# Hybrid DeltaNet / short-conv layer: where block 0 keeps its modulation sums, its later modulation rows and its decay vectors

## The chip, the cores and the metric

One core of a Trainium2 chip runs the whole layer. The metric is the time of one execution on the device in microseconds (us), as the median of three runs. Engines are named as in the profile: PE (TensorE matmul), PEld (its weight load), DVE (VectorE), ACT (ScalarE), POOL (GpSimd) and SP (SyncE, which here only issues DMAs). "L158" is line 158 of the kernel before; "SPq" is SP's queue of DMA issues.

## The reference, cut to what matters

Sequence 2048, width 1024, one layer, float32. `c` is one conditioning row, and from it come six modulation rows:

```
mod = silu(c) @ w_ada + b_ada                      # (6 * 1024): shift, scale, gate for mixer and MLP
h = rmsnorm(x, pre_mix) * (1 + sc_m) + sh_m
proj = h @ w_in                                    # q,k,v,z of 4 heads, a, b, and three short-conv parts
q,k,v = silu(causal_conv4(.)); q,k l2-normed
g = -exp(dn_a_log) * softplus(a + dn_dt_bias); beta = sigmoid(b)
o = gated delta rule in chunks (triangular inverse per chunk, then a scan over chunks)
y = concat(rmsnorm(o) * silu(z), s_b * causal_conv3(s_c * s_h)) @ w_out
x = x + g_m * rmsnorm(y, post_mix)
h = rmsnorm(x, pre_ffn) * (1 + sc_f) + sh_f
x = x + g_f * rmsnorm(square(relu(h @ w_ff1)) @ w_ff2, post_ffn)
```

`w_ada` is 1024 x 6144, 25 MB: the six parts of 4 MB are shift, scale and gate of the mixer (parts 0, 1, 2) and of the MLP (parts 3, 4, 5).

## The kernel before, in words

The sequence is cut into four blocks of 512 tokens. Each block runs the opening norm with the transposition to feature-major (`pre_norm`, for block 0 `pre_norm_first`), the gating vectors (`gating`), the mixer (`mixer`, `mix_out`) and the MLP (`ffn`). Every matmul operand is split into a high and a low part (ACT casts the high part, line 246; DVE, sometimes POOL, subtracts for the low part, line 247), and each product is three matmuls (lines 332 and 337).

Weights of a projection pass through a staging tile `w1s` (`stage()`, three buffers of 512 KB), are split into `w1h` (three buffers) and used. In block 0 the split weights are also written to DRAM (`wc`), so that later blocks load them without a split.

The modulation exists only in block 0. There `silu(c) @ w_ada` is not a matmul at first: 128 rows of `w_ada` at a time are scaled by the column of `c_act` that belongs to them and summed on DVE, eight tiles to one sum (lines 127/129 and 156/158), and the sum over the 128 partitions is then taken by matmuls with a vector of ones (line 168, in `ada_affine`) or a matrix of ones (line 188, in `ada_gate`).

- Parts 0 and 1 are read in four quarters of 256 features (`ada_load`, line 146): quarters 0 and 2 into `sb` tiles, 1 and 3 into `w1h` tiles. `ada_first` sums a quarter in a `t2` tile. `t2` has four buffers, and the copies of `h` on their way to the split (line 268, released by line 272 on POOL) rotate through the same four. After each quarter `ada_affine` makes scale and shift, `to_hT` transposes two 128-feature tiles of `x`, and `proj` takes these two tiles into the accumulators of the four projections that are begun early (`EARLY`, 96 matmuls in all). The 16 matmuls of `gating` (lines 443, 445) come after.
- Parts 2, 4 and 3 are read in the mixer by `ada_acc`, eight rows of 512 KB each, through the same three `w1s` buffers as the projection weights (line 125); their sums live in `gate_m`, `gate_f` and one `sb` tile. Part 5 follows in the MLP of block 0, group 1.

The decay vectors `dn_a_log` and `dn_dt_bias` and the 8 columns of `w_in` for a and b are loaded from SP's queue behind the x tiles and the first two quarters (lines 371, 374, 377). `neg_a` (lines 485, 486) is computed from the first.

The chunk inverse in the mixer is a chain of 60 DVE instructions (lines 635, 637) between line 630 and line 640; its result goes through DRAM (`rd`) to the tile `comp`, from which `block_inverse` (matmuls of lines 667 to 689) starts, and then the scan.

`w2h` (pool `opnd`, three buffers of 512 KB) holds split `w_out` weights in `mix_out`, and in the MLP of block 0, groups 1 and 2, the pairs of `w_ff2` rows from which `weight_sums` makes sums for DRAM (lines 901 to 907). `wt` (pool `small`, two buffers) is a tile of `block_inverse`.

Buffers, semaphores and the order of instructions on each engine are set by a planner from the program order and its own estimate of times: an instruction can be put well ahead of its place in the program if its inputs and a buffer are free by that estimate. Once set, each engine and SP's queue run in that order and wait in it.

Of the kernel before, what the change touches and what calls it, by code (L numbers as in the profile page):

```python
# [8 lines left out]
F32 = mybir.dt.float32  # L9
F32R = mybir.dt.float32r  # L10
# [5 lines left out]
P = 128  # L16
SEQ = 2048
DM = 1024
KT = DM // P
DFF = 4096  # L20
TB = 512
NB = SEQ // TB
NT = TB // P
NH = 4
# [4 lines left out]
OFF_Z, OFF_AB, OFF_SB, OFF_SC, OFF_SH = 1536, 2048, 2056, 2568, 3080  # L29
# [3 lines left out]
def hybrid_layer(  # L33
# [21 lines left out]
    nc = tc.nc  # L55
    V, A, G, T = nc.vector, nc.scalar, nc.gpsimd, nc.tensor
    x, out = x[0], out[0]
    w_ada, w_in, w_out, w_ff1, w_ff2 = w_ada[0], w_in[0], w_out[0], w_ff1[0], w_ff2[0]

    const = ctx.enter_context(tc.tile_pool(name="const", bufs=1))  # L60
    big = ctx.enter_context(tc.tile_pool(name="big", bufs=1))
    opnd = ctx.enter_context(tc.tile_pool(name="opnd", bufs=2))
    work = ctx.enter_context(tc.tile_pool(name="work", bufs=2))
    small = ctx.enter_context(tc.tile_pool(name="small", bufs=2))
# [12 lines left out]
    def slot_a(dtype=F32):  # L77
        return big.tile([P, 1024], dtype, name="sa", bufs=15)

    def slot_b(dtype=F32):  # L80
        return big.tile([P, 1024], dtype, name="sb", bufs=7)

    def t2():
        return work.tile([P, TB], F32, name="t2", bufs=4)

    def stage():
        return work.tile([P, 1024], F32, name="w1s", bufs=3)

    def junk(n, ph):
        return work.tile([P, n], BF16, name="jk_" + ph, bufs=1)  # L90

# [29 lines left out]
    def ada_acc(part, acc):  # L121

        for k in range(KT):
            st = stage()
            nc.sync.dma_start(out=st, in_=w_ada[k * P:(k + 1) * P, part * DM:(part + 1) * DM])
            if k == 0:
                V.tensor_scalar(out=acc, in0=st, scalar1=c_act[:, 0:1], scalar2=None, op0=ALU.mult)
            else:
                V.scalar_tensor_tensor(out=acc, in0=st, scalar=c_act[:, k:k + 1], in1=acc,
                                       op0=ALU.mult, op1=ALU.add)  # L130
        return [acc[:, 0:TB], acc[:, TB:DM]]

    def ada_load(qd):

        if qd % 2:
            sts = []
            for _ in range(2):
                w = opnd.tile([P, 2, KT, P], F32R, name="w1h", bufs=3).bitcast(F32)
                w = w.rearrange("p a k f -> p a (k f)")
                sts += [w[:, 0], w[:, 1]]  # L140
        else:
            sts = [slot_b() for _ in range(4)]
        for k0, st in zip(range(0, KT, 2), sts):
            for n in range(2):
                c0 = n * DM + qd * 256
                nc.sync.dma_start(out=st.rearrange("p (k n f) -> p k n f", k=2, n=2)[:, :, n],
                                  in_=w_ada[k0 * P:(k0 + 2) * P, c0:c0 + 256]
                                  .rearrange("(k p) f -> p k f", p=P))
        return sts

    def ada_first(sts):
        acc = t2()
        for k in range(KT):
            sj = sts[k // 2][:, (k % 2) * TB:(k % 2 + 1) * TB]
            if k == 0:
                V.tensor_scalar(out=acc, in0=sj, scalar1=c_act[:, 0:1], scalar2=None, op0=ALU.mult)
            else:
                V.scalar_tensor_tensor(out=acc, in0=sj, scalar=c_act[:, k:k + 1], in1=acc,  # L158
                                       op0=ALU.mult, op1=ALU.add)
        return [acc[:, 256:512], acc[:, 0:256]]  # L160
# [67 lines left out]
    def meansq(src):  # L228
        s = small.tile([P, 1], F32, name="ss_w", bufs=8)
        A.activation(out=junk(DM, "w")[:, :src.shape[-1]], in_=src, func=AF.Square,  # L230
                     scale=float(DM) ** -0.5, accum_out=s)
        return s

    def load_x(b, t):
        t0 = b * TB + t * P
        xt = slot_a()
        nc.sync.dma_start(out=xt, in_=x[t0:t0 + P, :])
        return xt
# [113 lines left out]
    ]  # L352
    for r0, n, src in segs:
        nc.scalar.dma_start(out=rows[r0:r0 + n, :], in_=src)
    xn0 = [load_x(0, t) for t in range(NT)]
    quarters = [ada_load(0)]
    cols = const.tile([P, 109], F32, name="cols")
# [9 lines left out]
    dn_w = cols[:, 108:109]  # L367

    quarters.append(ada_load(1))
    alog = const.tile([P, NH], F32, name="alog")  # L370
    nc.sync.dma_start(out=alog, in_=dn_a_log.broadcast_to([P, NH]))
    neg_a = const.tile([P, NH], F32, name="neg_a")
    dtb = const.tile([P, NH], F32, name="dtb")
    nc.sync.dma_start(out=dtb, in_=dn_dt_bias.broadcast_to([P, NH]))

    wab_s = t2()[:, 0:64].rearrange("p (k f) -> p k f", k=KT)
    nc.sync.dma_start(out=wab_s, in_=w_in[:, OFF_AB:OFF_AB + 8].rearrange("(k p) f -> p k f", p=P))
    wab = const.tile([P, KT, 16], F32R, name="wab")
    V.tensor_copy(out=wab[:, :, 0:8], in_=wab_s)
    V.tensor_tensor(out=wab[:, :, 8:16], in0=wab_s, in1=wab[:, :, 0:8], op=ALU.subtract)  # L380
# [2 lines left out]
    for t in range(NT):  # L383
        A.activation(out=junk(DM, "w"), in_=xn0[t], func=AF.Square, scale=float(DM) ** -0.5,
                     accum_out=r0[:, 0, t:t + 1])
# [511 lines left out]
    def weight_sums(g, j, e, o):  # L897


        r0 = (g * GRP + 2 * j) * P  # L900
        nc.sync.dma_start(out=e, in_=w_ff2[r0:r0 + P, :])
        nc.sync.dma_start(out=o, in_=w_ff2[r0 + P:r0 + 2 * P, :])
        a, b = slice(0, TB), slice(TB, 2 * TB)
        V.tensor_tensor(out=e[:, a], in0=e[:, b], in1=e[:, a], op=ALU.subtract)
        V.tensor_tensor(out=e[:, b], in0=o[:, b], in1=e[:, b], op=ALU.subtract)
        V.tensor_tensor(out=o[:, b], in0=o[:, b], in1=e[:, a], op=ALU.subtract)
        V.tensor_tensor(out=o[:, a], in0=o[:, a], in1=o[:, b], op=ALU.subtract)
        for i, t in enumerate((e, o)):
            pend.append((sums[g][:, j, 2 * i:2 * i + 2, :], t.rearrange("p (i f) -> p i f", i=2)))

    def ffn(b, hT, x1d):
# [22 lines left out]
        for g in range(NG):  # L934
# [11 lines left out]
            def job():  # L946
                if jobs:
                    if g == 0:
                        e, o = slot_b(), slot_b()
                    else:  # L950
                        e, o = [opnd.tile([P, 2, TB], F32R, name="w2h", bufs=3).bitcast(F32)
                                .rearrange("p a f -> p (a f)") for _ in range(2)]
                    weight_sums(*jobs.pop(0), e, o)

            def relu2(ps, a, c0, c1):
# [44 lines left out]
            if b == 0 and g == 1:  # L1000
                ada_acc(5, ada["gate_f"])
# [43 lines left out]
            while jobs:  # L1045
                job()
# [4 lines left out]
            if g == NG - 1 and b == NB - 1:  # L1051
                combine()
                w2 = [[], []]
                for n in range(2):
                    ns = slice(n * TB, (n + 1) * TB)
                    for fp in range(HP):
                        r0 = (f0 + 2 * fp) * P
                        st = stage().rearrange("p (j f) -> p j f", j=2)
                        nc.sync.dma_start(out=st, in_=w_ff2[r0:r0 + 2 * P, ns]
                                          .rearrange("(j p) f -> p j f", p=P))  # L1060
                        for j in range(2):
                            i = n * GRP + 2 * fp + j
# [20 lines left out]
            if seven:  # L1083
                for an, bn, key in (("A11", "B11", "1"), ("S2", "T2", "6"), ("A12", "B21", "2"),
# [3 lines left out]
                    for d in range(HP // 2):  # L1088
# [8 lines left out]
                        for j in range(2):  # L1097
                            i = 2 * d + j
# [5 lines left out]
            else:  # L1104
                for n in range(2):
                    ns = slice(n * TB, (n + 1) * TB)
                    pss = [ps_acc() for _ in range(NT)]
                    for fp in range(HP):
                        r0 = (f0 + 2 * fp) * P
                        w = load_w2(w_ff2[r0:r0 + 2 * P, ns].rearrange("(j p) f -> p j f", p=P))  # L1110
                        for j in range(2):
                            f = 2 * fp + j
# [52 lines left out]
```

## Time and profile before

| | |
|---|---|
| median of 3 runs | 2547.3 us (2545.57 to 2550.13) |
| profiled execution, its own time | 2542.68 us |
| its span, first to last instruction | 2540.9 us |
| mean granted TensorE clock | 0.985 |
| PE busy | 2434.5 us (96%), 11874 matmuls |
| DVE / ACT / POOL busy | 1779.2 us (70%) / 1152.9 us (45%) / 225.2 us (9%) |
| DMA moved | 449.53 MB, mean 177 GB/s |

The profile is read from this one execution. PE's busy time is wide because matmuls are pipelined; where PE does nothing, something else sets the pace, so the table is read together with the stretches below: the busy time of each engine in a stretch, the granted clock, the share of the 16 DMA engines in use.

### The profile page before, as it was taken

The numbers are of one execution on the slowest core, as the hardware profiler recorded it, in microseconds if no ns is written. First come the engines' busy times: TensorE is split into PE (matmuls) and PEld (weight loads), VectorE is DVE, ScalarE is ACT, GpSimd is POOL, SyncE is SP. The second block draws the span as 40 slices with busy tenths as digits, with TensorE's granted clock in tenths as the row PEclk, the third lists the DMA queues.
The fourth block names the chain that finished last, engine by engine and source line by source line (L and its number), as shares of the span: only waits on it lengthen the run. The fifth ranks groups of instructions, "written<-read, shape, count | busy, mean of one in ns | idle before, by whom it ended". The sixth has DMA issues, their size and how long they took to land.

```text
span 2540.9 us, 33780 instructions
## 1 busy us (share of the span) xinstructions
PE 2434.5 (96%) x11874; PEld 2020.3 (80%) x11874; DVE 1779.2 (70%) x3833; ACT 1152.9 (45%) x2386; POOL 225.2 (9%) x391
## 2 busy tenths in 40 slices
PE   4886999999989999999999999999999999999998
PEld 3675887888868888888877898888887888888887
DVE  5677776777796568666688557856779556857675
ACT  4631563344555145544464244654455414654432
POOL 1312100000040110000002020000002020000000
PEclk8898999999999999999999999999999999999999
DMA  7378858975455642444556545155445554244453
GB/s 250 124 243 261 305 179 298 304 257 165 150 198 215 207 158 100 132 127 135 154 183 232 170 151 187 67 155 150 146 158 210 185 188 166 92 151 131 125 162 103
DMA packets 297268, 449.53 MB, mean 177 GB/s; under 512 B 39189, under 2 KB 195978, under 8 KB 282250
## 3 DMA queue, kind: packets, MB, share of 16 engines
q1 hardware_dynamic: 296912, 447.31, 53.6%
q8 instruction: 94, 1.54, 0.2%
q14 instruction: 76, 0.62, 0.1%
q10 hardware_dynamic: 186, 0.06, 0.0%
HBM read 376.01 MB, written 71.30 MB: 176 GB/s over the span
## 4 chain that ended last, share of the span: by engine, by line
PE 77%; DVE 13%; DMA 5%; ACT 3%; issue 2%; SPq 0%; ACTq 0%; POOL 0%; DVEq 0%
PE acc L332 43%; PE acc L337 24%; DVE t L435 2%; DVE w1h L247 1%; DMA w1s<-in_w_ada_dram 1%; PE pd L701 1%; DVE sa L506 1%; DMA w2h<-in_w_ff_dram 1%; PE pd L557 1%; PE pd L332 1%; PE tp L689 1%; DVE sb L847 1%; PE pd L715 1%; PE tp L677 1%; DVE t L158 1%
## 5 line engine op out<-in xcount | busy, mean ns | idle before, releaser
L332 PE MATMUL acc<-h,w1h 128*128 128x512 f32 x5184 | 1231.6, 394 | 18.2 <-ACT w1h L246 16.0
L332 PEld LDWEIGHTS acc<-h,w1h 128*128 128x128 f32 x5184 | 973.0, 189 | 218.4 <-ACT w1h L246 17.1
L337 PE MATMUL acc<-w1h,sa 128*128 128x512 f32 x2556 | 593.6, 391 | 3.9 <-ACT w1h L246 3.2
L337 PEld LDWEIGHTS acc<-w1h,sa 128*128 128x128 f32 x2556 | 478.6, 188 | 104.7 <-ACT w1h L246 3.6
L247 DVE TENSOR_TENSOR w1h<-w1s,w1h 128x1024 fp32r<-128x1024 f32 x333 | 406.8, 1222 | 146.8 <-ACT w1h L246 146.6
L246 ACT CAST w1h<-w1s 128x1024 fp32r<-128x1024 f32 (+1 forms) x343 | 359.1, 1047 | 308.6 <-PE acc L337 205.1
L957 DVE TENSOR_TENSOR t<-t 128x512 f32<-128x512 f32 (+1 forms) x148 | 91.4, 620 | 182.9 <-ACT t L956 180.1
L956 ACT ACTIVATE t<-acc 128x512 f32<-128x512 f32 (+1 forms) x132 | 73.8, 559 | 247.9 <-PE acc L332 247.5
L272 POOL TENSOR_TENSOR h<-t,h 128x256 fp32r<-128x256 f32 x70 | 56.4, 810 | 1250.4 <-ACT h L271 1245.7
L435 DVE SCALAR_TENSOR_TENSOR t<-cb,cols,t 128x512 f32<-128x512 f32 x144 | 118.7, 831 | 67.9 <-ACT t L433 65.8
L247 DVE TENSOR_TENSOR w2h<-sa,w2h 128x512 fp32r<-128x512 f32 x128 | 87.7, 687 | 38.6 <-ACT w2h L246 37.9
L332 PE MATMUL acc<-h,sa 128*128 128x256 f32 (+1 forms) x672 | 104.8, 313 | 7.2 <-ACT h L271 5.8
L332 PEld LDWEIGHTS acc<-h,sa 128*128 128x128 f32 x672 | 93.2, 199 | 15.6 <-ACT h L271 7.8
L246 ACT CAST w2h<-sa 128x512 fp32r<-128x512 f32 x128 | 78.4, 619 | 56.5 <-DVE w2h L247 35.4
L337 PE MATMUL acc<-w2h,sa 128*128 128x512 f32 x420 | 101.4, 393 | 0.0
L922 DVE TENSOR_TENSOR sb<-acc,sb 128x512 f32<-128x512 f32 x148 | 96.3, 681 | 2.0 <-PE acc L337 2.0
L337 PE MATMUL acc<-w2h,sb 128*128 128x512 f32 x384 | 91.5, 393 | 1.5 <-DVE sb L839 0.8
L337 PEld LDWEIGHTS acc<-w2h,sa 128*128 128x128 f32 x420 | 77.7, 188 | 15.6
L337 PEld LDWEIGHTS acc<-w2h,sb 128*128 128x128 f32 x384 | 71.2, 188 | 19.7 <-DVE sb L839 2.5
L246 ACT CAST sa<-t 128x256 fp32r<-128x256 f32 (+1 forms) x145 | 70.4, 486 | 23.6 <-DVE t L957 23.3
L247 DVE TENSOR_TENSOR sa<-t,sa 128x256 fp32r<-128x256 f32 (+2 forms) x145 | 75.2, 519 | 3.9 <-ACT sa L246 1.4
L230 ACT ACTIVATE jk_w<-sb 128x512 bf16<-128x512 f32 x64 | 40.3, 630 | 57.6 <-DVE sb L873 30.0
(285 smaller groups left out, 2738.0 us busy)
## 6 DMA issues: line engine op xcount, KB each, us to landing
w1s<-in_w_ff_dram SPq DMA_DIRECT2D x213, 512.0 KB, 3.9
w1h<-wc SPq DMA_DIRECT2D x86, 1024.0 KB, 4.9
w1s<-ws SPq DMA_DIRECT2D x112, 512.0 KB, 3.7
wc<-w1h SPq DMA_DIRECT2D x30, 1024.0 KB, 7.8
sa<-in_x_dram SPq DMA_DIRECT2D x32, 512.0 KB, 4.2
w1s<-in_w_in_dram SPq DMA_DIRECT2D x32, 512.0 KB, 5.8
w1s<-in_w_ada_dram SPq DMA_DIRECT2D x32, 512.0 KB, 4.7
sa<-in_w_out_dram SPq DMA_DIRECT2D x32, 512.0 KB, 5.2
```

The lines of the kernel that those rows point to most:

```text
L158: V.scalar_tensor_tensor(out=acc, in0=sj, scalar=c_act[:, k:k + 1], in1=acc, op0=ALU.mult, op1=ALU.add)
L230: A.activation(out=junk(DM, "w")[:, :src.shape[-1]], in_=src, func=AF.Square, scale=float(DM) ** -0.5, accum_out=s)
L246: A.copy(out=hi, in_=src)
L247: eng.tensor_tensor(out=lo, in0=src, in1=hi, op=ALU.subtract)
L272: (G if j or eng is A else V).tensor_tensor(out=hT[k][:, 1, cs], in0=tmp, in1=hT[k][:, 0, cs], op=ALU.subtract)
L332: T.matmul(out=ps[:, c0:c1], lhsT=w[a][:, k, :], rhs=hT[k][:, b, c0:c1], start=(k == 0 and n == 0), stop=(k == KT - 1 and n == 2))
L337: T.matmul(out=ps, lhsT=lhs[a], rhs=rhs[b], start=(start and n == 0), stop=(stop and n == 2))
L435: V.scalar_tensor_tensor(out=tmp, in0=cb[:, w:w + TB], scalar=conv_w[:, w, ft:ft + 1], in1=tmp, op0=ALU.mult, op1=ALU.add)
L506: V.tensor_tensor(out=rg[:, n], in0=bc(tri[:, None, :], [P, NH, P]), in1=bc(gh[:, n, t, :, None], [P, NH, P]), op=ALU.mult)
L922: V.tensor_tensor(out=accs[key], in0=ps, in1=accs[key], op=ALU.add)
L956: A.activation(out=a[:, c0:c1], in_=ps[:, c0:c1], func=AF.Relu)
L957: V.tensor_tensor(out=a[:, c0:c1], in0=a[:, c0:c1], in1=a[:, c0:c1], op=ALU.mult)
```

## The change

Three edits, all in block 0.

1. `ada_first` takes its sum in a `wt` tile (two buffers, otherwise used only by `block_inverse`) instead of a `t2` tile.
2. `ada_acc` (parts 2, 4, 3 and 5, 32 rows of 512 KB) loads into `w2h` buffers through a new helper `stage_w2h` instead of `w1s`. The `weight_sums` loads of groups 1 and 2 use the same helper, with the tiles they had.
3. The loads of `dn_a_log`, `dn_dt_bias` and the a/b columns of `w_in` are issued from ACT's queue, right behind the small row loads there, instead of from SP's queue behind quarter 1. Their `t2` tile is allocated earlier accordingly.

```diff
+    def stage_w2h():
+        t = opnd.tile([P, 2, TB], F32R, name="w2h", bufs=3)
+        return t.bitcast(F32).rearrange("p a f -> p (a f)")
+
@@ ada_acc
-            st = stage()
+            st = stage_w2h()
             nc.sync.dma_start(out=st, in_=w_ada[k * P:(k + 1) * P, part * DM:(part + 1) * DM])
@@ ada_first
-        acc = t2()
+        acc = small.tile([P, 2, 256], F32, name="wt", bufs=2).rearrange("p j i -> p (j i)")
@@ behind the small row loads, ahead of xn0 and ada_load(0)
     for r0, n, src in segs:
         nc.scalar.dma_start(out=rows[r0:r0 + n, :], in_=src)
+    alog = const.tile([P, NH], F32, name="alog")
+    nc.scalar.dma_start(out=alog, in_=dn_a_log.broadcast_to([P, NH]))
+    neg_a = const.tile([P, NH], F32, name="neg_a")
+    dtb = const.tile([P, NH], F32, name="dtb")
+    nc.scalar.dma_start(out=dtb, in_=dn_dt_bias.broadcast_to([P, NH]))
+    wab_s = t2()[:, 0:64].rearrange("p (k f) -> p k f", k=KT)
+    nc.scalar.dma_start(out=wab_s, in_=w_in[:, OFF_AB:OFF_AB + 8].rearrange("(k p) f -> p k f", p=P))
     xn0 = [load_x(0, t) for t in range(NT)]
     quarters = [ada_load(0)]
...
     quarters.append(ada_load(1))
-    alog = const.tile([P, NH], F32, name="alog")
-    nc.sync.dma_start(out=alog, in_=dn_a_log.broadcast_to([P, NH]))
-    neg_a = const.tile([P, NH], F32, name="neg_a")
-    dtb = const.tile([P, NH], F32, name="dtb")
-    nc.sync.dma_start(out=dtb, in_=dn_dt_bias.broadcast_to([P, NH]))
-
-    wab_s = t2()[:, 0:64].rearrange("p (k f) -> p k f", k=KT)
-    nc.sync.dma_start(out=wab_s, in_=w_in[:, OFF_AB:OFF_AB + 8].rearrange("(k p) f -> p k f", p=P))
@@ job() in ffn
                     else:
-                        e, o = [opnd.tile([P, 2, TB], F32R, name="w2h", bufs=3).bitcast(F32)
-                                .rearrange("p a f -> p (a f)") for _ in range(2)]
+                        e, o = stage_w2h(), stage_w2h()
```

## Rows read from the trace of the kernel before

**Rows 1.** Busy time by stretch: us (and instructions) per engine, clock, DMA share, GB/s.

```profile
183.00:238.00 55.00, 37.91 (x151) 29.44 (x150) 42.13 (x89) 9.61 (x14) 6.64 (x10) 0.84 0.87 271
366.00:545.00 179.00, 170.69 (x850) 143.09 (x849) 135.56 (x244) 73.67 (x138) 7.27 (x8) 0.98 0.88 302
545.00:2541.00 1996.00, 1968.10 (x9611) 1639.08 (x9609) 1387.48 (x3051) 913.73 (x1875) 144.84 (x277) 1.00 0.48 157
```

**Rows 2.** Waits of DVE, 0 to 85 us: total, times, longest.

```profile
DVE t L156 <- POOL h L272: 15.0, 3, 5.2
```

**Rows 3.** DVE in order of time, opening: start, us, line, what [idle before <-releaser].

```profile
21.71 0.17 DVE L486 TENSOR_SCALAR neg_a<-neg_a 128x4 f32<-128x4 f32 x1 [6.05 <-ACT neg_a L485]
...
24.82 1.22 DVE L247 TENSOR_TENSOR sa<-w1s,sa 128x1024 fp32r<-128x1024 f32 x1
25.96 0.74 DVE L158 SCALAR_TENSOR_TENSOR t<-sb,c_act,t 128x512 f32<-128x512 f32 x1
31.83 0.93 DVE L156 TENSOR_SCALAR t<-w1h,c_act 128x512 f32<-128x512 f32 x1 [5.13 <-POOL h L272]
...
36.88 3.11 DVE L158 SCALAR_TENSOR_TENSOR t<-w1h,c_act,t 128x512 f32<-128x512 f32 x4
...
53.84 1.53 DVE L158 SCALAR_TENSOR_TENSOR t<-sb,c_act,t 128x512 f32<-128x512 f32 x2
...
60.97 8.18 DVE L158 SCALAR_TENSOR_TENSOR t<-w1h,c_act,t 128x512 f32<-128x512 f32 x7
```

**Rows 4.** PE in order of time, opening.

```profile
45.93 10.31 PE L332 MATMUL acc<-h,sa 128*128 128x512 f32 x36 [1.86 <-ACT h L271]
...
60.75 7.05 PE L332 MATMUL acc<-h,sa 128*128 128x512 f32 x24 [2.07 <-ACT h L271]
69.30 1.02 PE L168 MATMUL tp<-ones,t 128*128 128x1 f32 x8 [1.50 <-DVE t L158]
...
83.75 0.39 PE L445 MATMUL tp<-h,wab 128*8 128x512 f32 x1
```

**Rows 5.** SP's DMA issues in order of time, opening.

```profile
16.45 0.34 SPq L371 DMA_DIRECT2D alog<-in_dn_a_log_dram  x1
...
18.48 1.12 SPq L293 DMA_DIRECT2D w1s<-in_w_in_dram  x1
```

**Rows 6.** Stretches around the landing of the decay vectors, columns as in rows 1.

```profile
18.00:20.00 2.00, 0.00 (x0) 0.00 (x0) 0.00 (x0) 0.00 (x0) 0.00 (x0) 1.00 1.09 384
20.00:22.00 2.00, 0.00 (x0) 0.00 (x0) 0.29 (x2) 0.20 (x1) 0.00 (x0) 1.00 1.08 247
```

**Rows 7.** Waits of PE, 183 to 240 us.

```profile
PE acc L332 <- ACT w1h L246: 16.0, 2, 14.4
```

**Rows 8.** SP's DMA issues in the mixer.

```profile
209.28 5.73 SPq L293 DMA_DIRECT2D w1s<-in_w_in_dram  x3
```

**Rows 9.** DVE groups, 85 to 316 us: count, busy us, mean ns, idle before.

```profile
L129 DVE SCALAR_TENSOR_TENSOR gate_m<-w1s,c_act,gate_m 128x1024 f32<-128x1024 f32 x7 | 9.0, 1282 | 5.6 <-DMA w1s<-in_w_ada_dram 5.5
L129 DVE SCALAR_TENSOR_TENSOR gate_f<-w1s,c_act,gate_f 128x1024 f32<-128x1024 f32 x7 | 8.9, 1272 | 1.4 <-DMA w1s<-in_w_ada_dram 1.4
```

**Rows 10.** DVE: first instruction of the inverse and the copy behind it, blocks 0 and 1.

```profile
183.06 0.68 DVE L630 TENSOR_SCALAR sa<-sa 64x1024 f32<-64x1024 f32 x1
...
224.03 1.11 DVE L640 COPY sa<-sa 64x1024 f32<-64x1024 f32 x1
...
842.42 0.69 DVE L630 TENSOR_SCALAR sa<-sa 64x1024 f32<-64x1024 f32 x1 [10.62 <-DMA sa<-ud]
...
868.07 1.13 DVE L640 COPY sa<-sa 64x1024 f32<-64x1024 f32 x1
```

**Rows 11.** PE: block_inverse begins in block 0; projections ahead of it in block 1.

```profile
237.80 0.49 PE L667 MATMUL tp<-sa,bd 128*128 128x128 f32 x2
...
839.65 45.27 PE L332 MATMUL acc<-h,w1h 128*128 128x512 f32 x199
```

**Rows 12.** Chain of waits in the MLP of block 0: start, us, what.

```profile
504.05 6.44 DMA ws<-w2h
```

## Prediction
> **What bounds the kernel now.** I read the busy time by stretch first. From 545 us on PE is busy 1968.1 of 1996 us at full clock, so nothing is to be had there from block 0's edits [rows 1]. The loss is in the first 316 us. Between 183 and 238 us PE is busy 37.9 of 55 us at a clock of 0.84 while DVE has 42.1 us of work and the DMA share is 0.87 [rows 1]. For the opening (0 to 85 us) I then read DVE and PE in order of time: PE's first long run of matmuls starts at 45.93 and its last gating matmul ends at 84.14 [rows 4]. Before each run PE waits for a sum of a modulation quarter on DVE, and DVE itself sits idle in front of these sums [rows 2, 3]. Last I compared block 0's inverse with block 1's, where no modulation row is in the way [rows 10, 11].
>
> **The opening, step by step.** In DVE's order `neg_a` stands inside quarter 0's sum, and DVE is idle 6.05 us until it can run [rows 3]: it waits for `dn_a_log`, issued only at 16.45 behind x and two quarters [rows 5]. Issued on ACT's queue with the small rows this wait goes. What is late next is the split of the first early weights at 24.82, which stands between the last two steps of that sum [rows 3]. Its load is issued at 18.48, 2.0 us after the first of the three loads that leave SP [rows 5], so it can come at most about 2 us earlier. If the split keeps its place quarter 0's sum ends 2.0 us earlier (26.70 becomes 24.7); if it falls behind the sum, up to 6 us. I take 2.0, since the order follows from the planner's estimates, and its cause, the weights' arrival, hardly moves.
>
> Quarters 1, 2 and 3 each start after a wait of DVE for POOL's line 272, 15.0 us in three waits of which the first is 5.13 [rows 2, 3]: the sum needs a `t2` buffer that a copy of `h` still holds. With two `wt` buffers this wait goes. `wt` is free until `block_inverse`; a third sum needs the eight small matmuls of the first to be over, which come right after it. So, the steps themselves unchanged, quarter 1's sum ends at 39.99 - 2.0 - 5.1 = 32.9, quarter 2's at 55.37 - 12 = 43, quarter 3's at 69.15 - 17 = 52 [rows 3]. Quarter 2's and 3's loads need buffers that the sums of 0 and 1 give back, so they are issued earlier by as much.
>
> From there PE is late next. Its 36 matmuls start 5.9 us after quarter 1's sum (39.99 to 45.93) and end at 56.24 [rows 3, 4]; shifted by 7.1 they end at 49.1. Quarter 2's sum is there by 43, so its matmuls follow without a wait: before, that part took from 56.24 to 67.80, 11.6 us [rows 4], so it ends at 60.7. Quarter 3's part took from 69.30 to 84.14, 14.8 us [rows 4]: end at 75.5, 8.6 us earlier. In both parts PE waits some 2 us for the new `h` (2.07 is shown) and the sums are now there 6 to 9 us before PE needs them, so I add about 2.4 us of cover: **opening 11 us**. Bounds: 4 us if the DMA stream can't bring quarters and weights any earlier than by the waits at its head, 17 us if all the DVE waits are returned.
>
> The moved loads: three more issues on ACT at 0.34 us each [rows 5] stand ahead of ACT's first work, about 1 us, and ACT waits for x there anyway. Their small pieces cost the DMA stream: its rate was 384 GB/s just before and 247 GB/s in the 2 us in which they landed [rows 6], so (384 - 247) x 2 / 384 = 0.7 us. That is paid ahead of the x tiles now instead of ahead of the early weights: 0 to 0.7 us, inside the rounding of the 11.
>
> **The mixer, step by step.** PE's idle time between 183 and 240 us is one hole of 14.4 us (16.0 in two waits) for an ACT cast [rows 7]. The three projection weights that it needs are issued only at 209.28 [rows 8], because the eight rows of part 4 are in front of them in the three `w1s` buffers, and these are emptied by DVE instructions that stand between the steps of the inverse. With rows in `w2h` the weights have `w1s` for themselves and come while PE works on the ones before. What is late next is the inverse: its result starts `block_inverse` at 237.80 [rows 11], 13.8 us after line 640 [rows 10]. The inverse took 41.0 us (183.06 to 224.03) in block 0 and 25.7 in block 1 [rows 10]. Part 4's sums are 8.9 us in seven steps, 1.4 of wait and a first step of at most the 1.27 of the others: 10.3 to 11.6, say 11 us, of the 15.3 between the two [rows 9]. Since `w2h` and `gate_f` are free from the start, I expect these sums to be put well ahead, into the DVE and DMA gaps of the opening's end and the convolutions. Then the inverse ends 11 us earlier, and PE has the projections of the refilled `w1s` to fill that time; in block 1 it runs 199 matmuls through the same place without a gap [rows 11]. **Inverse 11 us**; bounds 0 (the sums stay where they are, and PE, without its hole, waits for `comp` instead) and 17.1 (all that PE is short of 55 us there, rows 1). Part 2's sums wait 5.6 us for rows ahead of the inverse [rows 9]; between 0 and 5.6 us I take **2**, as PE still has matmuls for most of it. Part 3's rows come while the scan starts; I count nothing, between -2 and 3.
>
> **The MLP of block 0.** Part 5's rows now rotate through `w2h` with the pairs for `weight_sums`. The stretch has a DMA share of 0.88, and PE is short of it by 8.3 us (179 - 170.7) [rows 1]. The bytes are the same. `w1s` is freed for the MLP weights, `w2h` gets tighter; from -5 to 5 I take 0. The cover is the sums' lead: they are for the next group.
>
> **Sum.** 11 + 11 + 2 = 24 us off 2542.7 (the profiled execution; span 2540.9 and 1.8 around it) gives 2518.7. That execution is 4.6 us under the median of the runs, 2547.3, and 24 off the median is **2523 us**.
>
> **The rivals.** *Only one of the two halves.* Either the sums of part 4 stay in the inverse, so PE waits for `comp` (opening and part 2: 13 us, 2534), or the rows are put into the opening and its loads wait for them (mixer alone: 13 us, 2534). For the second speaks that the stream is full there: 384 GB/s at a share of 1.09 [rows 6]; eight rows of 0.524 MB are 4.2 MB, or 11 us at that rate, all of the opening's gain. Against it, rows come behind all else in the program, so SP issues them only where it would wait. The Trainium skill has a rule for this half (DMA: Bandwidth & Descriptors, section "Issuing engines are not separate DMA queues"): DMAs of all queues run on the same 16 engines and interleave, and a second issuing engine saves issue time alone. By it a second staging tile makes no bandwidth either, and the opening's gain would be paid back as computed, for 2534; the rate that falls to 247 GB/s while the decay loads pass agrees.
>
> *All of it.* All DVE waits of the opening (17), all of PE's hole (17.1), all of part 2's wait (5.6): 40 us, 2507. For it: block 1 has no gap. Against it: the weights' split in quarter 0, and PE itself in the opening.
>
> *Hidden anyway.* PE-bound opening (4) and an inverse that is not shortened: 2543. That includes the case that the planner's new order brings new waits of the size of those that go, as `neg_a` was one.
>
> *Slower: SP blocked in the MLP.* In group 1 a `w2h` buffer of a pair is free again only after its store, 6.44 us [rows 12]. If SP's order puts each of part 5's eight rows in front of MLP weights, and each finds no free buffer, SP stands 8 x 6.4 = 51 us, and the weights behind it too. PE's lead is three staged weights of 24 matmuls each, at 7.05 us [rows 4] 21 us. PE then loses 30 us, and against a gain of 24 the kernel is 6 us slower, 2553. It decides from the eighth row: seven blocked rows (45 - 21 = 24) cancel the gain. For it: SP has one order and waits in it. Against it: `gate_f` is read for the last time in `mix_out`'s beginning, so the rows can be taken before the pairs fill `w2h`.
>
> **Chances.** Forecast 0.46 (own range 2513 to 2533), one half only 0.20, all of it 0.12, hidden anyway 0.09, slower 0.13. The time is that of the likeliest. The range runs from 2503 (the sum of the upper bounds, 17 + 17.1 + 5.6 + 3 = 43, off the median, and a little more) to 2550, which leaves out the slower half of the last case and little below. A difference under 0.2%, 5 us, can't be told from none by a measurement of this kernel. Faster by more than that: 0.46 + 0.20 + 0.12 and 0.02 of the hidden case = 0.80; within 0.07; slower 0.13.
>
> **What would show it.** Opening: no idle time of DVE before `neg_a`, none for POOL's line 272 before a quarter's first step, and the last gating matmul near 73 instead of 84.14. Mixer: part 2's and 4's sums before the inverse, line 640 some 30 us after line 630, the hole of 14.4 us gone, `block_inverse` some 24 us earlier than at 237.80. MLP: SP's waits ahead of part 5's rows of no consequence for PE. The prediction is wrong if rows of `w_ada` are issued before quarter 3's loads and DVE waits for them there, if part 4's sums still stand between the steps of the inverse, or if what is gained by 316 us is lost by 545.

## The result: 2503.1 us, and the profile after

The changed kernel takes **2503.1 us** (median of 4 runs, 2500.59 to 2507.84) beside 2546.4 us for the kernel before on the same chip (4 runs, 2545.15 to 2550.13): ratio 0.983, 95% interval 0.981 to 0.985. That is 43 us less, where the prediction's sum had 24. The profiled execution of the changed kernel took 2500.59 us, span 2498.9; all spans below are of one execution each.

Both kernels run the same 11874 matmuls, so the 42.0 us between the spans part cleanly: PE's busy time falls from 2434.5 to 2420.0 us (14.5 us: the same work at a higher clock) and its idle time from 106.4 to 78.9 us (27.5 us). That the 14.5 us are the clock can be checked: if the busy time of each stretch of 2 us is multiplied by the clock granted in it, the sums up to the first step of block 1's inverse are 730.9 us before and 731.2 after, while the busy times themselves are 755.6 and 741.0. The first line of the page after:

```profile
PE 2420.0 (97%) x11874; PEld 2011.8 (81%) x11874; DVE 1770.9 (71%) x3833; ACT 1149.2 (46%) x2384; POOL 235.1 (9%) x391
```

By stage, cut in both at the same places of the work (last gating matmul; first step of the inverse; end of the mixer's last `w2h,sb` matmuls; first step of block 1's inverse). Busy time by stretch, columns as in rows 1, first before, then after:

```profile
0.00:84.50 84.50, 47.31 (x178) 33.85 (x178) 40.86 (x77) 35.18 (x72) 18.11 (x27) 0.88 0.71 225
84.50:183.00 98.50, 88.30 (x397) 70.92 (x398) 76.93 (x157) 52.42 (x125) 28.13 (x39) 0.95 0.56 180
183.00:356.10 173.10, 150.21 (x795) 125.32 (x794) 128.42 (x283) 71.07 (x167) 26.80 (x40) 0.93 0.72 241
356.10:843.00 486.90, 469.75 (x2198) 385.95 (x2198) 364.62 (x723) 219.85 (x425) 41.07 (x55) 0.99 0.69 229
```

```profile
0.00:72.00 72.00, 42.95 (x178) 31.79 (x178) 40.20 (x78) 34.57 (x72) 20.88 (x27) 0.95 0.81 262
72.00:169.00 97.00, 83.45 (x392) 67.97 (x393) 82.19 (x167) 52.42 (x125) 40.56 (x39) 0.96 0.77 264
169.00:317.90 148.90, 146.52 (x801) 124.11 (x800) 115.39 (x273) 68.07 (x165) 20.78 (x40) 0.99 0.67 228
317.90:801.00 483.10, 468.05 (x2199) 383.89 (x2198) 364.89 (x722) 219.80 (x425) 41.07 (x55) 0.99 0.69 231
```

The length of a stretch less PE's busy time in it is PE's idle time. The opening is 12.5 us shorter, 8.1 of it idle time and 4.4 busy time. The stage of the convolutions is 1.5 us shorter; its idle time grows by 3.3. The inverse, the scan and `w_out` are **24.2 us shorter**, 20.5 of it idle time. The MLP and the head of block 1 are 3.8 us shorter. The counts of matmuls per stage differ by six at most.

What answers to rows 4, 7, 10 and 11, PE and DVE in order of time:

```profile
71.31 0.39 PE L448 MATMUL tp<-h,wab 128*8 128x512 f32 x1
...
160.47 64.42 PE L336 MATMUL acc<-h,w1h 128*128 128x512 f32 x283
224.73 0.38 PE L670 MATMUL tp<-sa,bd 128*128 128x128 f32 x2
```

```profile
168.93 0.68 DVE L633 TENSOR_SCALAR sa<-sa 64x1024 f32<-64x1024 f32 x1
...
204.91 1.14 DVE L643 COPY sa<-sa 64x1024 f32<-64x1024 f32 x1
...
800.58 0.69 DVE L633 TENSOR_SCALAR sa<-sa 64x1024 f32<-64x1024 f32 x1 [10.92 <-DMA sa<-ud]
```

The last gating matmul ends at 71.7 (84.14 before, [rows 4]). The hole of 14.4 us [rows 7], a stretch in which PE does nothing, is gone: 283 projection matmuls run without a gap from 160.47 to `block_inverse`, which starts 13.1 us earlier than before [rows 11], where the prediction had some 24. The inverse takes 36.0 us (41.0 before, [rows 10]), where the prediction had some 30: the sums are gone from it, but a second short convolution's steps (2.6 us) and a wait of 2.9 us for a weight's cast now stand in it. So the mixer's gain does not come through an earlier `block_inverse` alone: more projections are done ahead of it, and 54 projection matmuls are left behind its start in this stage, where there were 145.

The groups of rows 9, 40 to 165 us, all ahead of the inverse now:

```profile
L133 DVE SCALAR_TENSOR_TENSOR gate_m<-w2h,c_act,gate_m 128x1024 f32<-128x1024 f32 x7 | 11.1, 1585 | 4.1 <-DMA w2h<-in_w_ada_dram 4.1
L133 DVE SCALAR_TENSOR_TENSOR gate_f<-w2h,c_act,gate_f 128x1024 f32<-128x1024 f32 x7 | 8.9, 1277 | 0.3 <-DMA w2h<-in_w_ada_dram 0.3
```

And DVE in the opening, which answers to rows 3 (the lines of `wt` are the first steps of quarters 0, 1 and 3):

```profile
14.09 0.19 DVE L382 CAST wab<-t 128x64 fp32r<-128x64 f32 x1 [11.74 <-DMA t<-in_w_in_dram]
...
14.74 0.16 DVE L489 TENSOR_SCALAR neg_a<-neg_a 128x4 f32<-128x4 f32 x1
...
15.90 0.49 DVE L160 TENSOR_SCALAR wt<-sb,c_act 128x512 f32<-128x512 f32 x1
...
22.84 0.48 DVE L160 TENSOR_SCALAR wt<-w1h,c_act 128x512 f32<-128x512 f32 x1
...
42.80 0.48 DVE L160 TENSOR_SCALAR wt<-w1h,c_act 128x512 f32<-128x512 f32 x1
```

No sum waits for POOL's line 272 any more [rows 2], nor for `neg_a`. A new wait stands at the head: DVE idles 11.74 us for the a/b columns, now first in its order. PE has one new hole, 8.8 us in front of pair 0's tail. (The heads are taken in two pairs; a pair's tail, `pair_tail`, finishes the norms of its q and k on DVE and runs the matmuls that need them.) The wait of PE, 85 to 240 us:

```profile
PE tp L578 <- DVE bco L544: 8.8, 1, 8.8
```

### The profile page after: what moved, and what is told of

Read it like the earlier page. It is cut to its first block, busy times and chain, and to the rows that moved or that the text cites. A ratio compares the mean times of both kernels' runs of the same rounds, so it can differ in the third digit from the quotient of the medians.

```text
span 2498.9 us, 33774 instructions
## 1 busy us (share of the span) xinstructions
PE 2420.0 (97%) x11874; PEld 2011.8 (81%) x11874; DVE 1770.9 (71%) x3833; ACT 1149.2 (46%) x2384; POOL 235.1 (9%) x391
## 4 chain that ended last, share of the span: by engine, by line
PE 76%; DVE 13%; DMA 6%; ACT 2%; issue 2%; POOL 0%; SPq 0%; ACTq 0%; DVEq 0%
PE acc L336 43%; PE acc L341 24%; DVE t L438 1%; DVE w1h L251 1%; DMA w2h<-in_w_ada_dram 1%; PE pd L704 1%; DMA ws<-w2h 1%; DMA w2h<-in_w_ff_dram 1%; DVE sa L509 1%; PE pd L560 1%; PE pd L336 1%; DMA sb<-in_w_ff_dram 1%; DVE sb L925 1%; PE tp L692 1%; PE tp L680 1%
```

## The experiments

The times stand beside one another, each with its ratio to the kernel before on the same chip. Differences in the text are worked out from the ratios, times 2546.4 us, since the kernel before itself came out 3 us apart from chip to chip (2543.3 to 2546.4). PE busy and idle are of the profiled execution (idle is span less busy); "mixer's end" is the start of the last `w2h,sb` matmul of block 0.

| kernel | us | ratio, 95% | PE busy | PE idle | mixer's end |
|---|---|---|---|---|---|
| before | 2546.4 | 1 | 2434.5 | 106.4 | 355.7 |
| all three edits | 2503.1 | 0.983 (0.981-0.9849) | 2420.0 | 78.9 | 317.5 |
| e1_wt: edit 1 | 2528.6 | 0.9938 (0.9923-0.9952) | 2431.0 | 95.8 | 339.4 |
| e2_w2h: edit 2 | 2516.4 | 0.9892 (0.9875-0.9909) | 2425.1 | 90.1 | 329.0 |
| e3_queue: edit 3 | 2543.8 | 0.9998 (0.9988-1.0007) | 2428.5 | 106.9 | 351.2 |
| e12: edits 1, 2 | 2503.8 | 0.9838 (0.9821-0.9855) | 2424.8 | 74.4 | 311.9 |
| e13: edits 1, 3 | 2534.9 | 0.9959 (0.9944-0.9974) | 2431.2 | 103.8 | 346.6 |
| l1_late: all, later sums after both pair tails | 2520.1 | 0.9906 (0.989-0.9923) | 2425.7 | 91.0 | 333.8 |
| l0_late: all, later sums after pair 0's tail | 2526.0 | 0.9921 (0.9907-0.9936) | 2436.4 | 88.0 | 339.2 |
| l4: all, part 4's sums after pair 0's tail | 2511.8 | 0.9867 (0.9853-0.9881) | 2424.3 | 85.4 | 324.0 |
| e13ns: e13 without seven steps of part 4 | 2550.3 | 1.0019 (1.0008-1.003) | 2438.2 | 113.9 | 362.1 |
| wabsp: all, a/b columns back on SP | 2502.7 | 0.983 (0.9814-0.9846) | 2424.5 | 76.5 | 316.7 |
| e12g2: e12, part 5 a group later | 2502.6 | 0.9832 (0.9819-0.9846) | 2422.6 | 74.5 | 312.9 |
| e12s4: e12, four `w1s` tiles | 2501.8 | 0.9836 (0.9822-0.9849) | 2424.0 | 77.4 | 316.1 |

**e1_wt**, `acc = t2()` becomes the `wt` tile, nothing else.

> The kernel before with the first edit alone: the quarters' sums in wt. Theory A (three edits whose effects add: the opening's waits, the decay vectors' wait, and projection weights freed from the modulation rows): the three waits of DVE for POOL's line 272 go, the 6 us before neg_a stay, the last gating matmul ends 6 to 9 us before 84.14, the rest of the kernel only shifts: 2537 to 2541. Theory C (the edits work through one another, since the planner orders everything anew): the opening gains less than 3 us alone, 2543 to 2548.

It takes 15.8 us off (12 to 20), more than either theory. The last gating matmul ends at 67.0, 17.2 us earlier than before and 4.7 earlier than with all three edits. The hole in the inverse stays. PE in order of time, then three stretches in and behind the hole, columns as in rows 1:

```profile
169.85 17.78 PE L332 MATMUL acc<-h,w1h 128*128 128x512 f32 x70 [0.53 <-DVE w1h L247]
...
202.11 1.22 PE L332 MATMUL acc<-h,w1h 128*128 128x512 f32 x2 [14.48 <-ACT w1h L246]
203.92 17.83 PE L332 MATMUL acc<-h,w1h 128*128 128x512 f32 x70 [0.58 <-DVE w1h L247]
```

```profile
190.00:195.00 5.00, 0.00 (x0) 0.00 (x0) 5.00 (x8) 0.26 (x1) 0.00 (x0) 0.54 0.81 228
205.00:210.00 5.00, 5.00 (x18) 3.99 (x17) 4.39 (x11) 0.07 (x1) 0.00 (x0) 0.75 0.89 310
215.00:220.00 5.00, 5.00 (x24) 4.13 (x22) 2.68 (x4) 0.00 (x0) 0.73 (x3) 1.00 0.76 165
```

This is how a hole's second price is read: in it the granted clock is 0.54 and 0.50 (half speed, 1.2 GHz), and the first 5 us in which PE is fully busy again (205 to 210) do 18 matmuls, where 24 fit at full clock.

**e2_w2h**, `ada_acc` takes `stage_w2h()`, nothing else (the loads of `weight_sums` keep the `w2h` tiles they had).

> The kernel before with the second edit alone: modulation rows in w2h. Theory A: the opening stays at 84 us, all that is gained behind it is there: 28 to 31 us, 2515 to 2519, and PE has no hole between the inverse's start and block_inverse. Theory B, that of the prediction (the inverse sets the mixer, and is shorter by the sums that leave it): 13 us, 2533. Theory C: under 8 us alone.

It takes 27.5 us off: theory A, by the time; the opening is not the same, as the last gating matmul ends at 88.1, 3.9 us later. PE is busy without a gap at full clock from 165 to 225, and the inverse takes 30.4 us:

```profile
165.00:225.00 60.00, 60.00 (x274) 49.83 (x273) 47.59 (x108) 16.77 (x24) 9.66 (x16) 1.00 0.90 274
```

Of the 25.7 us between the spans 16.3 are idle time and 9.4 busy time.

**e3_queue**, the three loads on ACT's queue, nothing else.

> The kernel before with the third edit alone: decay vectors and a/b columns on ACT's queue. Theory A: the 6 us before neg_a go, but the head starts 2 us later (DVE waits for the a/b columns until about 14 us) and the waits for line 272 stay: 0 to 4 us off, 2542 to 2546. Theory C: slower than before by 2 us or more, as the head's loss stays without the gains behind it.

There is no difference that can be measured (theory A, by the time). `neg_a` no longer waits, but the a/b columns and the weights' split do. Waits of DVE, 0 to 85 us:

```profile
DVE wab L378 <- DMA t<-in_w_in_dram: 11.8, 1, 11.8
DVE sa L247 <- ACT sa L246: 9.0, 1, 9.0
...
DVE t L156 <- POOL h L272: 6.0, 2, 4.1
```

**e13**, edits 1 and 3, and **e12**, edits 1 and 2.

> The kernel before with edits 1 and 3, without edit 2 (later rows in the weights' staging, as before). Theory A (edits add up): 2546 less 17.5 (edit 1 alone) less 0.5 (edit 3 alone), 2527 to 2530; a hole of about 14 us on ACT's split of w1h stays, and block_inverse starts near 222 as with edit 1 alone. Theory B (edit 3 costs 4 to 5 us once edit 1 has taken the wait for POOL away): 2531 to 2534. Either way it is 6 us or more behind the kernel with rows in w2h but the sums held back to the pair tails (2520), which is then the worth of the free staging without the moved sums.

> The kernel before with edits 1 and 2 (running sums in the scan's tile, rows in w2h), without edit 3 (alog, dtb and the a/b columns stay on SP behind the second quarter). With edit 1 alone the last modulation column came at 48.9 us, with all three edits at 53.6 us. Theory A (edit 3 costs in the opening: the columns' load holds DVE 11.7 us at the head and slows SP's first issues): the column comes near 49 again, the mixer starts some 4 us earlier and the time is 2497 to 2501. Theory B (edit 3 is neutral, as it measured alone): 2502 to 2505, the column earlier but the start of block_inverse within 1 us of 224.7.

Without edit 2, edit 3 costs 5 us (ratio 0.9959 against 0.9938): nearest to theory B of e13, with intervals that overlap, so that it costs anything is likely and not shown. On top of both others it changes nothing that can be told apart (0.9838 without, 0.983 with), though without it the gating ends at 67.3 instead of 71.7 and the mixer 5.6 us earlier. That is the time of e12's theory B, but not its reason, as `block_inverse` starts at 220.8, 3.9 us earlier. The lead is gone when block 1 starts. On the way, in the MLP, PE waits once more for a split weight and the clock is lower. The wait and the stretch of e12:

```profile
PE acc L341 <- ACT w1h L250: 4.1, 1, 4.1
```

```profile
330.00:400.00 70.00, 62.54 (x353) 55.41 (x352) 51.08 (x108) 25.44 (x53) 3.00 (x4) 0.90 0.85 293
```

**wabsp**, of the three loads only the columns' goes back to SP.

```diff
-    nc.scalar.dma_start(out=wab_s, ...)
     ...
+    nc.sync.dma_start(out=wab_s, ...)   # behind the second quarter
```

> The changed kernel with one of edit 3's three loads moved back: the a/b columns (1024 pieces of 32 bytes) on SP behind the second quarter, alog and dtb still on ACT's queue. Theory A (the columns' load is what edit 3 costs): no 11.7 us wait of DVE at the head, SP's x issues back from 6.4 to 4.6 us, the first quarter's sum from 13.6 instead of 15.9 us, the last modulation column near 49 to 50 instead of 53.6 us, and the time 2497 to 2501. Theory B (the 11.7 us are slack, since the first quarter sets the start): the time within 1.5 us of 2503.

The 11.7 us wait goes and the time stays: theory B. The opening does not return either (gating ends at 72.1), because x and the first quarter still come late: DVE waits 3.7 us for the quarter's tile and starts its sum at 14.68 (15.90 with all three edits, 11.98 in e12). SP's issues of x and of the first quarter, first wabsp, then e12:

```profile
1.27 6.13 SPq L241 DMA_DIRECT2D sa<-in_x_dram  x4
7.44 6.16 SPq L150 DMA_DIRECT2D sb<-in_w_ada_dram  x8
```

```profile
1.27 4.66 SPq L241 DMA_DIRECT2D sa<-in_x_dram  x4
5.98 4.63 SPq L150 DMA_DIRECT2D sb<-in_w_ada_dram  x8
```

So what delays the opening is not the columns' load alone: with only the two loads of 2 KB on ACT's queue, 16 bytes to each of 128 partitions, it is as late.

**l1_late**: the changed kernel, but the sums of parts 2 to 5 read a copy of `c_act` that is made after both pair tails, so they stand in the inverse again while their rows stay in `w2h`. **l0_late**: the same with the copy made behind pair 0's tail.

```diff
@@ ada_acc (the first step, k = 0, likewise; the making of the copy ada["c"] is left out here)
-                V.scalar_tensor_tensor(out=acc, in0=st, scalar=c_act[:, k:k + 1], in1=acc,
+                V.scalar_tensor_tensor(out=acc, in0=st, scalar=ada["c"][:, k:k + 1], in1=acc,
```

> The kernel after, but the sums of parts 2, 4 and 3 (and 5) read a copy of c_act that is made behind the last pair tail (one tiny DVE instruction), so that part 4's sums stand between the steps of the inverse again while their rows still load into w2h. The inverse takes about 40 us again. Theory A: PE has the projections of a free w1s to run through, so block_inverse's delay costs little: within 5 us of after, 2500 to 2508; it may even win, as no sum stands in the convolutions. Theory B: block_inverse and all behind it come 11 us later, 2512 to 2516.

> The changed kernel with the sums of parts 2 and 4 held back until pair 0's tail (they read a copy of c_act that is made there). DVE's order then has part 2's sums and two of part 4's ahead of the inverse, six of part 4's inside it. In the changed kernel none is inside it (2503), and with all of part 4's and three of part 2's inside (2520) it cost 17 us. Theory A (the sums between the inverse's steps hold up DVE's half of the weights' splits, so PE starves, in proportion): six of eleven, 9 us of 17, 2510 to 2514, with holes of 6 to 9 us on w1h's split in the inverse. Theory B (what counts is the hole ahead of pair 0's tail, 8.8 us at 123 to 132, which goes): 2495 to 2501. Theory C (no matter where, if the stagings are free): 2503 within 2.

l1_late is 19 us slower than the changed kernel, slower than both its theories, and 13 faster than e13, which has the sums at about the same place and its rows in `w1s`. l0_late fits none of its three theories: it is at least as slow as l1_late. Its theories counted sums of parts 2 and 4 alone, but six of part 3's (`sb`) stand in the inverse too. From 165 to 225 us DVE spends 20.9 us on sums in l1_late and 18.1 in l0_late, 7.1 in the changed kernel. The inverse takes 43.1 and 50.6 us and PE has waits of 14.0 and 13.4 us for split weights. Waits of PE, 85 to 330 us, first l1_late, then l0_late:

```profile
PE acc L336 <- ACT w1h L250: 8.3, 2, 5.7
PE acc L336 <- DVE w1h L251: 5.7, 2, 4.5
```

```profile
PE acc L336 <- ACT w1h L250: 6.9, 3, 3.4
PE acc L336 <- DVE w1h L251: 6.5, 2, 4.5
```

The trace of l1_late shows how sums on DVE reach PE although `w1s` is free. Between 165 and 225 us SP stands 18.2 us in nine waits for DVE before it can issue rows into `w2h`, and the stores of split weights (`wc<-w1h`), which give the `w1h` tiles back, stand behind these rows in its order. ACT then waits for a store before it can cast the next weight, once 12.9 us, and PE for ACT. Waits of ACT, 150 to 225 us, first the changed kernel, where ACT waits mostly for PE to give a tile back and never for a store, then l1_late; last SP's issues in l1_late ahead of the longest wait:

```profile
ACT w1h L250 <- PE acc L336: 12.2, 3, 4.4
```

```profile
ACT w1h L250 <- DMA wc<-w1h: 21.3, 3, 12.9
```

```profile
179.82 1.82 SPq L129 DMA_DIRECT2D w2h<-in_w_ada_dram  x2
181.70 0.42 SPq L288 DMA_DIRECT2D wc<-w1h  x1
```

**l4**: only part 4's sums are held back, to pair 0's tail.

> The changed kernel with part 4's sums alone held back until pair 0's tail (they read a copy of c_act made there; part 2's stay where they are). DVE's order has all eight sums of part 4 between pair 0's tail and the inverse. Theory A (PE's hole of 8.8 us at 123 to 132 us comes from sums of part 4 ahead of pair 0's norms): the hole shrinks by the 3.3 us of the three steps there or more, the mixer ends 3 to 5 us earlier, PE's idle time falls from 78.9 to 74 to 76 us, and the time is 2497 to 2501. Theory B (given back behind the mixer, as in the kernel without edit 3, where an earlier end of the mixer by 5.6 us left the time at 2503.8): mixer's end 3 to 5 us earlier, time 2502 to 2505, with a new hole or a lower granted clock between 330 and 400 us. Theory C (the sums slip into the inverse after all): 2508 to 2520.

The hole falls to 6.9 us, and nothing is gained: the kernel is 9 us slower, `block_inverse` starts at 227.6, PE waits 5.0 us for a weight in the MLP, and the clock is lower (0.91 from 85 to 165 us, 0.95 from 225 to 330, where the changed kernel has 0.96 and 0.98). None of the theories holds; why the mixer ends 6.5 us later is not settled.

**e13ns**: e13 with steps 1 to 7 of part 4's sums replaced by a copy of 8 columns, so that the kernel leaves part of the MLP's gate out and what it returns is not the layer's output.

```diff
+            elif part == 4:
+                V.tensor_copy(out=acc[:, 8 * k:8 * k + 8], in_=st[:, 0:8])
```

> The kernel before with edits 1 and 3, and with steps 1 to 7 of part 4's sums left out: each row is still loaded into the weights' staging, and a copy of 8 columns reads it in place of the 1.27 us step (so the gate of the MLP is not computed from part 4's rows). It parts the two things that edit 2 does: free staging and sums that leave the inverse. Measured so far: rows in the staging and sums in the inverse 2534.9, staging free and sums in the inverse 2520.1, both gone 2503.1. Theory A (DVE's sums between the inverse's steps are half of it or more: they hold up DVE's part of the weights' splits and give the staging back late): the inverse takes 33 to 35 us instead of 43.1, the hole of 14.6 us on w1h's split shrinks under 6 us, PE's idle time falls from 103.8 to some 92 us and the time is 2510 to 2521. Theory B (the rows in the staging are what counts, since the weights' loads stand behind eight rows of 0.5 MB): a hole of 10 us or more stays, 2526 to 2533.

The inverse is short, 29.2 us, and the kernel is 15 us *slower* than e13, outside both theories. DVE, then PE, in order of time:

```profile
173.18 0.69 DVE L631 TENSOR_SCALAR sa<-sa 64x1024 f32<-64x1024 f32 x1
...
202.33 1.02 DVE L641 COPY sa<-sa 64x1024 f32<-64x1024 f32 x1
```

```profile
204.25 14.46 PE L334 MATMUL acc<-h,w1h 128*128 128x512 f32 x48 [10.88 <-ACT w1h L248]
...
278.39 3.04 PE L778 MATMUL tp<-ident,sa 128*128 128x128 f32 x8 [12.08 <-DVE sa L772]
```

The hole on `w1h` stays at 10.9 us as theory B said. `block_inverse` starts 6 us earlier than in e13, with 175 projection matmuls between 160 us and its start instead of 196. At the scan's end PE then stands 12.1 us for DVE, with a granted clock of 0.50 from 270 to 285 us, and runs 140 projection matmuls in a row afterwards. Part of these 12.1 us is no price of a short inverse: in the new order seven of part 3's sums stand ahead of and between the steps of the norm that PE waits for (8.4 us of DVE; in e13 all eight are over by 262 us). So the run shows that a shorter inverse with the rows in `w1s` gains nothing here; how much the new place of part 3's sums costs in it is open. Six of them, DVE groups, 262 to 279 us:

```profile
L131 DVE SCALAR_TENSOR_TENSOR sb<-w1s,c_act,sb 128x1024 f32<-128x1024 f32 x6 | 7.7, 1282 | 0.6 <-DMA w1s<-in_w_ada_dram 0.6
```

**e12g2**: e12 with `ada_acc(5)` called at group 2 instead of 1. **e12s4**: e12 with four `w1s` tiles instead of three.

> The kernel with edits 1 and 2 (2503.8; its mixer ends 5.6 us earlier than that of the changed kernel, its block 1 starts at the same time) and with part 5's rows called for one group later in the MLP of block 0. In that kernel PE has a hole of 4.1 us on w1h's split at 385 us and a granted clock of 0.91 between 320 and 400, at a DMA share of 0.85 to 0.90. Theory A (the MLP's beginning is bound by the weights' transfers, and part 5's 4.2 MB, 13.5 us at 310 GB/s, stand among them): the hole goes, the clock there is 0.96 or more, and the time is 2496 to 2500. Theory B (the rows fill gaps; the hole is the weights' own start after an earlier mixer): hole and clock as before, 2502 to 2505.

> The kernel with edits 1 and 2 (2503.8) and four staging tiles for the weights instead of three. Its mixer ends 5.6 us earlier than the changed kernel's, and PE then waits 4.1 us in the MLP of block 0 for a split of a weight (w1h), at a lower granted clock; calling part 5's rows later left the time at 2502.6 and a wait of 2.9 us. Theory A (the three staging tiles still set how early a weight can come; each is given back only after both halves of the split): the wait in the MLP goes, the clock between 330 and 400 us is 0.96 or more, PE's idle time falls from 74.4 to some 70 us, and the time is 2494 to 2500. Theory B (the transfers themselves are the limit there, at a DMA share of 0.85 to 0.90, whatever the staging): the wait stays within 1 us of 4, 2501 to 2506. Theory C (a fourth tile lets weights run ahead of rows that are needed sooner): the sums of parts 2 and 4 come later, and the time is over 2506.

Both end within 2 us of the changed kernel: no version beats it beyond what can be told apart. Both have the time of their theory B. In e12g2 the clock from 320 to 400 us rises to 0.98, as theory A wanted, and the time stays. e12s4 has an inverse of 48.5 us, with all eight of part 3's sums in it. It ends 15.9 us later than in the changed kernel, and PE has no gap beside it:

```profile
172.32 0.68 DVE L634 TENSOR_SCALAR sa<-sa 64x1024 f32<-64x1024 f32 x1 [2.02 <-DMA sa<-ud]
...
220.84 1.12 DVE L644 COPY sa<-sa 64x1024 f32<-64x1024 f32 x1
```

```profile
165.00:225.00 60.00, 60.00 (x266) 49.72 (x266) 49.91 (x99) 15.46 (x21) 5.50 (x6) 1.00 0.89 295
```

Its waits for split weights in the MLP come to 4.1 us, now for DVE's half of the split, so there neither the count of stagings (e12s4) nor part 5's rows (e12g2, 2.9 us left) is all of it. What is, stays open.

## Why the prediction was right in direction and short in size

The time fell inside the stated range, 2503 to 2550, by 0.1 us; two of the four runs lie below it, and the forecast's own range, 2513 to 2533, was missed by 10 us. That is luck. The lower end was reached as the sum of upper bounds "and a little more" (2547.3 - 42.7 is 2504.6), and that sum left out the 5 us that the text allowed for the MLP. The gain also came in other places than the sum had it, as follows.

**Opening, 11 us predicted: 12.4 measured**, by errors that cancel. Edit 1 alone gives 17.2 us, the upper bound of the text: with two free sums the planner moves `neg_a` out of quarter 0's sum by itself, so edit 3 had no wait left to remove. The moved loads, priced at 0 to 0.7 us, cost 4.4 there (71.7 against 67.3). The row read for them [rows 6] was of a stream that already ran, and of loads on SP's own queue; at the head, the stream falls to 105 GB/s in the 2 us from 8 to 10, against 365 before. The Trainium skill (DMA: Bandwidth & Descriptors, section "Issuing engines are not separate DMA queues") says that transfers issued from several engines share the same 16 DMA engines; the 4.66 us of SP's x issues that became 6.13 and 6.42 agree. The rival built on it (rows of part 2 pay the opening back, 2534) did not come about: the first row is issued at 43.34 us, behind quarter 3's loads. And 4.4 us of the stage's gain are busy time, which the sum did not count. One reading was too wide: PE waited for a quarter's sum ahead of quarters 0, 1 and 3, but quarter 2's sum was over at 55.37, before PE had finished at 56.24 [rows 3, 4].

**Part 2, 2 us predicted: 1.7** (12.4 at the gating, 14.1 at line 633). DVE's 5.6 us of waits for rows [rows 9] became 4.1, and PE got the hole of 8.8 us; the stage is 1.5 us shorter in all.

**"Inverse 11 us": about 24 measured. This step failed**, in its size and in its reason. The text took the inverse as what is late once the hole is gone, and so gave the hole's 17.1 us only as a bound. But a shorter inverse with the hole left (e13ns) is slower, and a longer one without it (e12s4) is as fast. What sets the time there is whether split weights reach PE. In seven kernels rows do not hold the weights' staging and DVE spends 3 to 10 us on sums between 165 and 225 us: e2_w2h, e12, e12s4 (the most, 9.6), e12g2, wabsp, l4 and the changed one. In all of them PE is busy for all of these 60 us. In l1_late and l0_late, with 18 us of sums and more, it is not; in l1_late the wait goes through SP's queue, as shown there. With PE busy, a later `block_inverse` costs little, because projections run ahead of it that would otherwise run behind it. Both halves of edit 2 are needed: free staging is worth 13 us (e13 to l1_late), the sums' place 19 more (l1_late to the changed kernel). Part 4's sums taken out alone gain nothing (e13ns, 15 us slower than e13, in part by another order of part 3's sums).

**The clock was priced at nothing.** The row of 183 to 238 us showed a granted clock of 0.84 beside the 37.9 us of busy time [rows 1], and the opening has 0.88 (the first stretch above); only the idle time was counted. The other 14.5 us are the same matmuls in less time. In idle time alone the sum looks close, 24 predicted and 27.5 measured, but that is luck too: by stage it was 11 against 8.1, 2 against -3.3, 11 against 20.5 and 0 against 2.1.

**MLP, 0 predicted: 3.6 to 3.8 better.** The rival in which SP is blocked there did not come: from 320 to 545 us no single wait of PE is longer than 1.0 us, where before there was one of 3.2.

*Only one half* and *Hidden anyway* fell. *All of it* (2507) came nearest in time, for another reason: it counted the opening's 17 us, of which edit 3 gives back 4, and no clock.

## What to carry to other kernels

Price a hole of PE twice: its length, and the lower clock in which the work behind it runs; a changed kernel with the same instructions lets both be read apart, as idle and busy time of PE. Where PE has work that may go before or after a serial chain, as the projections here, the length of that chain need not be the bound: ask which queue feeds PE beside it, and what stands in that queue in front of a load or of a store that gives a buffer back. And price a load moved to the head of another queue at the head, where the first tiles come in, not by a row of the full stream.

## What was not expected of the hardware

A DVE instruction with two SBUF inputs of 128x512 takes 0.74 to 0.75 us, but 2.91 us where POOL runs its half of a weight's split on 128x1024 beside it. DVE, then POOL, in the changed kernel:

```profile
117.42 2.91 DVE L438 SCALAR_TENSOR_TENSOR t<-cb,cols,t 128x512 f32<-128x512 f32 x1
120.25 0.16 DVE L200 TENSOR_SCALAR rs_z_d<-ssq 128x16 int32<-128x16 int32 x1
120.36 0.75 DVE L438 SCALAR_TENSOR_TENSOR t<-cb,cols,t 128x512 f32<-128x512 f32 x1
```

```profile
117.39 2.39 POOL L251 TENSOR_TENSOR w1h<-w1s,w1h 128x1024 fp32r<-128x1024 f32 x1
```

The Trainium skill (Trainium Architecture — The Big Picture, section "What this means for kernel authors") says that DVE and GpSimd share a port pair under an exclusive lock. The rows agree, as the DVE instruction ends 0.55 us after POOL's; they do not tell a lock from another way of sharing. Another of 2.86 us follows at 126.93, again beside POOL, so these two alone are 4.3 us longer than at 0.75, ahead of pair 0's tail and its hole of 8.8 us; whether the hole would be shorter without them was not tried.
